# A hybrid decoder layer on one core: the low part of k over zeros, and linear-attention outputs grouped by tiling

## The chip, the cores and the metric

One of the eight cores of a Trainium2 chip runs the whole kernel. The metric is the device time of one execution in microseconds (us); less is better. TensorE (PE) does the matrix products and its weight loads (PEld), VectorE is DVE, ScalarE is ACT, GpSimd is POOL, and SyncE (SP) issues most DMAs.

## What is computed

One layer on 512 tokens of width 1024 in float32: a norm, three token mixers side by side, a gated sum of them, an output projection, and a feed-forward part. Two mixers matter here. Stick-breaking attention (8 heads of 64) and gated linear attention (4 heads, keys of 64, values of 128, chunks of 64 tokens). The attention takes 128 query tokens at a time, with the keys up to their end:

```python
def stick_breaking_attention(q, k, v):
    for i in range(seq // SB_BLOCK):
        ...
        z = jnp.einsum('bhtd,bhsd->bhts', qb, kb) * scale
        ...
        log_1m = jnp.where(mask, jax.nn.log_sigmoid(-z), 0.0)
        tail = lax.cumsum(log_1m, axis=3, reverse=True) - log_1m
        w = jnp.where(mask, jnp.exp(jax.nn.log_sigmoid(z) + tail), 0.0)
        outs.append(jnp.einsum('bhts,bhsd->bhtd', w, vb))
...
def gla_chunked(q, k, v, log_a):
    attn = jnp.where(causal, jnp.einsum('bhntk,bhnsk->bhnts', q_dec, k_inv), 0.0)
    o_intra = jnp.einsum('bhnts,bhnsv->bhntv', attn, v)
...
    o_inter = jnp.einsum('bhntk,bhnkv->bhntv', q_dec, states_before)
    return (o_intra + o_inter).reshape(b, h, s, dv)
```

## The kernel before

Every large product is made of three: each float32 operand is split into a high and a low part of type float32r, and high times high, low times high and high times low are summed in one PSUM bank. Weights come in as 128 x 1024 pieces (512 KB), are split by ACT (line 95) and DVE (line 96), and are used one piece later. Products in plain float32 (transposes, linear attention) need no split; each of those that are not transposes shows in the trace as two records.

PE's program is written out by hand: a feed of projection products (lines 169 to 171 and 100 to 102, all with 128 rows of contraction, 128 stationary columns and 512 moving columns) is handed out piece by piece between the steps of the short chains that wait on other engines. `feed.pull(n)` puts n such products in between.

*The scores of the attention* (`weigh`, lines 589 to 607) run for 8 heads times 4 token blocks, so 32 times. A head has 64 features, half of the 128 rows. Tile `ab` holds, stacked along the rows, q high over q low, and k high twice, so the first product (line 594) makes q high · k high + q low · k high with all 128 rows. The second (line 595) adds q high · k low and uses only the 64 rows of its head (`own`). Block tb takes (tb+1)·128 moving columns, so the 32 steps have 8 each of 128, 256, 384 and 512 columns. Then ACT takes two sigmoids (598, 599), POOL masks (601), DVE runs the product along the keys (604) and one multiplication (606), and a step later PE transposes the result (`turn`, line 616). `k_done` (573 to 583) makes the low part of k of a pair of heads with one DVE subtraction over 128 partitions (579).

*The outputs of the linear attention* (`outputs`, 488 to 517) run four times. A call fills one bank with four pieces of 128 columns, j = 0 to 3 (two token blocks, two heads of the same half e). For each piece comes one product inside the chunks (line 495: 128 rows, 128 columns), and then one for each of its two chunks from the state (line 501: 64 rows, 64 stationary columns, into one half of the partitions). The first chunk of all has no state and is left out, so two calls have 6 products at line 501 and two have 8.

```python
mm(op_[:, o], ats[n0 // 2][:, 4 * e + j, :], gv[:, n, h * P:(h + 1) * P], start=True, stop=False, ...)
for c in (2 * n, 2 * n + 1):
    mm(op_[q0:q0 + 64, o], gq[r, i, c * 64:(c + 1) * 64], st_[r, i, c, :], start=False, stop=True, ...)
```

Small tiles of 128 x 512 float32 come from one pool `tmp` (tag `t2`) with 10 buffers; a scheduler that lays the program out gives a new tile any buffer that is free by then and moves a few instructions within an engine's order.

Of the kernel before, what the change touches and what calls it, by code (L numbers as in the profile page):

```python
# [9 lines left out]
F32 = mybir.dt.float32  # L10
F32R = mybir.dt.float32r
# [5 lines left out]
P = 128  # L17
# [11 lines left out]
class Feed:  # L29
    """Matrix products in the order in which they are to run, handed out piece by piece between the steps of  # L30
    the chains that wait on other engines. A unit is (name, load, body): load() brings the weights in, one
    unit ahead; body(weights) yields after each piece, saying for how many products of 512 columns it stands."""

# [33 lines left out]
def hybrid_layer_kernel(ctx: ExitStack, tc: tile.TileContext, a):  # L67
# [4 lines left out]
    xpool = ctx.enter_context(tc.tile_pool(name="xpool", bufs=1))  # L72
    tmp = ctx.enter_context(tc.tile_pool(name="tmp", bufs=10))
    small = ctx.enter_context(tc.tile_pool(name="small", bufs=6))
# [11 lines left out]

    # ---------------- weights: loaded as float32, split exactly into two float32r parts
    def weights(src, shape, name, parts=None, halves=False):
# [14 lines left out]

    # ---------------- while the first loads run: the activation table, and the tensor engine's clock
    warm = const.tile([P, S], mybir.dt.bfloat16, name="warm")
    nc.gpsimd.memset(warm, 0.0)
# [5 lines left out]

    # ---------------- constants
    g1 = const.tile([P, KD], F32, name="g1")
    nc.sync.dma_start(out=g1, in_=a["mix_pre_g"])

    # ---------------- x, feature-major, times the gain, split
    xTh = xpool.tile([P, KD, S], F32R, tag="aTh", name="xTh")
# [12 lines left out]
    def proj_tm(src, name, done, before=None):  # L131
        """x as the stationary operand: four banks of [128 tokens, 512 columns]."""
        banks = []
# [29 lines left out]
    def proj_fm(src, name, done):  # L163
        """the weights as the stationary operand: a bank of [128 columns, 512 tokens]."""
        def body(w):
            hi, lo = w
            out = bank("acc", f"{name}_ps")
            for k in range(KD):
                mm(out, hi[:, k, :], xTh[:, k, :], start=k == 0, stop=False)  # L169
                mm(out, hi[:, k, :], xTl[:, k, :], start=False, stop=False)  # L170
                mm(out, lo[:, k, :], xTh[:, k, :], start=False, stop=k == KD - 1)  # L171
                if k < KD - 1:
                    yield 3
            done(out)
            yield 3

        feed.add(name, lambda: weights(src, [KD, P], name), body)
# [14 lines left out]

    # ---------------- 1/rms of x: per token-partition, and along the free axis
    ss = small.tile([P, 2, NB], F32, tag="ss1", bufs=1, name="ss")
# [19 lines left out]
    with ExitStack() as mix:  # L214
# [6 lines left out]
        def transposed(src, yh, yl, n, name):  # L221
            """four [128 tokens, 128 features] of block n into the feature-major pair."""
            pt = bank("tv", f"{name}_t{n}")
            for k in range(4):
                nc.tensor.transpose(out=pt[:, k * P:(k + 1) * P], in_=src[k], identity=ident)
            ptv = pt.rearrange("p (k t) -> p k t", k=4)
            t = slice(n * P, (n + 1) * P)
            nc.scalar.activation(yh[:, :, t], ptv, AF.Copy)
            nc.vector.tensor_tensor(out=yl[:, :, t], in0=ptv, in1=yh[:, :, t].bitcast(F32), op=ALU.subtract)

        # ---------------- branch B: spatial gating
        big = mixer.tile([P, 2, NB, S], F32, tag="big", name="sg_uv")
# [21 lines left out]

        # ---------------- what branch C needs first: the low-rank gate, queries and keys
        gla = mix.enter_context(ExitStack())
        gp_ = gla.enter_context(tc.tile_pool(name="gla", bufs=1, side="right"))
        gbias = gp_.tile([P, 2], F32, name="gbias")
        nc.gpsimd.dma_start(out=gbias, in_=a["gla_b_gate"])
        # stacked along the contraction: hi, hi and lo parts of the weights against hi, lo and hi of the gate,  # L260
        # each twice for the two halves that the gate's own product comes in
        gupr = t2("gupr")
        gup = gp_.tile([96, 256], F32R, name="gup")
        for i in range(6):
# [3 lines left out]
                                op=ALU.subtract)  # L268
        # both parts of the low-rank weights side by side as the stationary operand
        gdw = gp_.tile([P, KD, 32], F32R, name="gdw")  # L270
# [44 lines left out]

        # the gate's logarithm, and its running sum in each chunk
        maskg = gp_.tile([P, P], I32, name="maskg")
# [20 lines left out]

        # ---------------- branch B: the spatial mixing
        for gp in range(4):  # L340
# [23 lines left out]

        # ---------------- branch C: gated linear attention
        nc.vector.tensor_tensor(out=la.rearrange("p i (c t) -> p (i c) t", t=64),
# [5 lines left out]
        nc.scalar.activation(dec, cumv[:, :, 63], AF.Exp, scale=1.0 / 16)  # L372
        # two token blocks at a time share one of these
        ats = [x.rearrange("p i (n s) -> p (i n) s", s=P) for x in (la, ex)]
# [18 lines left out]

        # ---------------- gated merge of a branch, two column tiles at a time
        macc = mixer.tile([P, KD, S], F32, tag="macc", name="macc")
# [57 lines left out]
        for i in range(2):  # L453
            # a bank for each of the two row tiles that the chunks' tokens lie in
            ups = [bank("att", f"up{i}{e}") for e in range(2)]
# [20 lines left out]
        def scores(n0):  # L476
            # a bank for each row tile that the heads' features lie in
            for e in range(2):
# [9 lines left out]
        def outputs(n0, e):  # L488
            r = slice(e * 64, e * 64 + 64)
            op_ = bank("att", f"op{n0}{e}")  # L490
            for j in range(4):
                n, i = n0 + j // 2, j % 2
                h = 2 * i + e
                o = slice(j * P, (j + 1) * P)
                mm(op_[:, o], ats[n0 // 2][:, 4 * e + j, :], gv[:, n, h * P:(h + 1) * P], start=True, stop=False,
                   skip_group_check=True)
                for c in (2 * n, 2 * n + 1):
                    if c == 0:
                        continue
                    q0 = (c % 2) * 64  # L500
                    mm(op_[q0:q0 + 64, o], gq[r, i, c * 64:(c + 1) * 64], st_[r, i, c, :],
# [39 lines left out]

        # ---------------- branch A: stick-breaking attention
        feed.to("wp1_3")
        yah, yal = yT("ya")
        with tc.tile_pool(name="attn", bufs=1, side="right") as ap:
# [10 lines left out]
            ab, kl, wts = {}, {}, {}  # L556

            def own_oth(h):
                e = h % 2
                return slice(e * 64, e * 64 + 64), slice(64 - e * 64, 128 - e * 64)  # L560

            # stacked along the contraction: [q hi; q lo] against [k hi; k hi], and q hi against k lo
            def q_done(pq, p):
# [9 lines left out]
            def k_done(pk, p):  # L573
# [3 lines left out]
                nc.scalar.activation(kh, kf, AF.Copy)  # L577
                kl[p] = ap.tile([P, S], F32R, tag="kl", bufs=2, name=f"kl{p}")
                nc.vector.tensor_tensor(out=kl[p], in0=kf, in1=kh.bitcast(F32), op=ALU.subtract)
                for h in (2 * p, 2 * p + 1):  # L580
# [8 lines left out]
            def weigh(h, tb):  # L589
                own, _ = own_oth(h)  # L590
                w = (tb + 1) * P
                t = slice(tb * P, w)
                z = bank("att", f"z{h}{tb}")
                mm(z[:, :w], ab[h][:, 0, t], ab[h][:, 1, :w], start=True, stop=False)
                mm(z[:, :w], ab[h][own, 0, t], kl[h // 2][own, :w], start=False, stop=True)  # L595
                beta = t2(f"be{h}{tb}")
# [90 lines left out]

        # ---------------- token-major residual, and what the FFN needs
        late = ctx.enter_context(tc.tile_pool(name="late", bufs=1, side="right"))
# [17 lines left out]
        with tc.tile_pool(name="mlo", bufs=1, side="right") as mlp:  # L707
# [5 lines left out]

            # ---------------- output projection, norm, residual, norm, transposed
            hTh = xpool.tile([P, KD, S], F32R, tag="aTh", name="hTh")
            hTl = xpool.tile([P, KD, S], F32R, tag="aTl", name="hTl")

            def inv_rms(srcs, junks, name):
# [3 lines left out]
                v = small.tile([P, 1], F32, tag="v2", name="v2" + name)  # L722
                # 1024 (mean + eps); the factor 32 is in the gains
                nc.vector.tensor_scalar(out=v, in0=s2[:, 0:1], scalar1=s2[:, 1:2], scalar2=D * EPS,
# [5 lines left out]
            def after_mixer(n, yb_):  # L730
                """norm and residual of token block n."""
                ys = [t2(f"h{n}{hf}") for hf in range(2)]
# [39 lines left out]

            # the last half of the contraction runs block after block, so that their norms start one by one
            wo = {}
# [36 lines left out]

            # the first pairs run on the first half of the tokens while the second half is still normalized
            first_ps = {fi: bank("acc" if fi[0] else "att", "up%d_ps%d" % fi) for fi in first}
# [7 lines left out]

    # ---------------- convolutional gated FFN
    ffn = ctx.enter_context(tc.tile_pool(name="ffn", bufs=1))
# [65 lines left out]
def _layouts(i):  # L889
    """The inputs as the kernel reads them: slices, transposes and reshapes only."""  # L890
    import numpy as np
# [47 lines left out]
```

## Time and profile before

| | |
|---|---|
| device time, median of 3 runs | 872.11 us (870.83 to 873.0) |
| profiled execution, span from first to last instruction | 872.2 us |
| PE busy | 861.5 us (99%) |
| PE weight loads, DVE, ACT, POOL busy | 698.2, 480.4, 355.8, 89.3 us |
| mean granted clock of PE | 0.997 of full speed |
| DMA | 86.45 MB, mean 99 GB/s |

The page gives no time of the profiled execution apart from its span, and that lies 0.1 us over the median of the runs. Matmuls overlap in the pipeline, so a matmul's own duration is longer than what it costs; the cost is the distance from its start to the start of the next. In the rows a form such as 64*128 is rows times columns of the stationary operand.

### The profile page before, as it was taken

How to read it: one execution, taken by the hardware profiler on the slowest of the kernel's cores; microseconds unless marked ns; L12 is line 12 of the kernel's file. 1: busy time of each engine (PE TensorE's matmuls, PEld its weight loads, DVE VectorE, ACT ScalarE, POOL GpSimd, SP SyncE). 2: the span in 40 equal slices, each digit the busy share in tenths (PEclk: the TensorE clock that was granted, in tenths of full speed). 3: DMA queues.
4: the chain of work that ended last, by engine and by line, in shares of the span. 5: the costliest groups of instructions: out<-in, count | busy, mean ns of one | idle time of the engine just before them, and what ended most of it. 6: DMA issues, size and time to landing. Idle time of an engine off the chain costs nothing.

```text
span 872.2 us, 10327 instructions
## 1 busy us (share of the span) xinstructions
PE 861.5 (99%) x4005; PEld 698.2 (80%) x4005; DVE 480.4 (55%) x652; ACT 355.8 (41%) x536; POOL 89.3 (10%) x137
## 2 busy tenths in 40 slices
PE   8999999999999999999999999999999999999996
PEld 5878877788887777777888898888888888888885
DVE  4358444544266777775664766666666666422225
ACT  6436223322256566554333435444444444311112
POOL 2210003000002332332100120000000000000001
PEclk9999999999999999999999999999999999999999
DMA  8522222122222122222525122232222222222212
GB/s 314 187 69 97 75 94 73 49 97 97 96 91 80 49 73 73 72 73 95 219 97 183 58 73 73 97 97 97 96 97 97 97 97 96 97 97 97 97 49 96
DMA packets 26192, 86.45 MB, mean 99 GB/s; under 512 B 3216, under 2 KB 3712, under 8 KB 26144
## 3 DMA queue, kind: packets, MB, share of 16 engines
q1 hardware_dynamic: 24624, 81.35, 27.2%
q0 software_dynamic: 1520, 4.45, 1.6%
q8 instruction: 31, 0.51, 0.2%
q14 instruction: 17, 0.14, 0.1%
HBM read 83.69 MB, written 2.10 MB: 98 GB/s over the span
## 4 chain that ended last, share of the span: by engine, by line
PE 98%; DMA 1%; SPq 0%; ACT 0%; DVE 0%; issue 0%; POOLq 0%; DVEq 0%; ACTq 0%
PE up_ps L808 9%; PE up_ps L809 9%; PE up_ps L810 9%; PE wg_ps L169 5%; PE wg_ps L171 5%; PE wg_ps L170 5%; PE dn L101 5%; PE dn L100 5%; PE dn L102 5%; PE pp L100 3%; PE pp L102 3%; PE pp L101 3%; PE wo L101 2%; PE wo L102 2%; PE wo L100 2%; PE z L595 1%
## 5 line engine op out<-in xcount | busy, mean ns | idle before, releaser
L809 PE MATMUL up_ps<-hTl,h_wup 128*128 128x512 f32 (+1 forms) x336 | 129.0, 384 | 0.0
L810 PE MATMUL up_ps<-hTh,l_wup 128*128 128x512 f32 (+1 forms) x336 | 129.0, 384 | 0.0
L808 PE MATMUL up_ps<-hTh,h_wup 128*128 128x512 f32 (+1 forms) x336 | 128.9, 384 | 0.0
L96 DVE TENSOR_TENSOR l_wup<-r_wup,h_wup 128x1024 fp32r<-128x1024 f32 x41 | 50.2, 1225 | 64.9 <-ACT h_wup L95 64.9
L169 PE MATMUL wg_ps<-xTh,h_wg 128*128 128x512 f32 x192 | 78.9, 411 | 0.0
L171 PE MATMUL wg_ps<-xTh,l_wg 128*128 128x512 f32 x192 | 75.2, 392 | 0.0
L170 PE MATMUL wg_ps<-xTl,h_wg 128*128 128x512 f32 x192 | 74.9, 390 | 0.0
L808 PEld LDWEIGHTS up_ps<-hTh,h_wup 128*128 128x128 f32 x336 | 63.0, 188 | 12.5
L810 PEld LDWEIGHTS up_ps<-hTh,l_wup 128*128 128x128 f32 x336 | 63.1, 188 | 12.4
L809 PEld LDWEIGHTS up_ps<-hTl,h_wup 128*128 128x128 f32 x336 | 63.1, 188 | 12.4
L96 DVE TENSOR_TENSOR l_wdn<-r_wdn,h_wdn 128x1024 fp32r<-128x1024 f32 x22 | 27.0, 1226 | 82.9 <-ACT h_wdn L95 82.9
L831 DVE SCALAR_TENSOR_TENSOR cv<-up_ps,cw,cv 128x511 f32<-128x511 f32 (+1 forms) x88 | 65.6, 747 | 7.8 <-ACT cv L829 6.2
L101 PE MATMUL dn<-l_wdn,guh 128*128 128x512 f32 x176 | 68.6, 390 | 0.0
L102 PE MATMUL dn<-h_wdn,gul 128*128 128x512 f32 x176 | 68.5, 389 | 0.0
L100 PE MATMUL dn<-h_wdn,guh 128*128 128x512 f32 x176 | 68.4, 389 | 0.0
L95 ACT ACTIVATE h_wdn<-r_wdn 128x1024 fp32r<-128x1024 f32 x22 | 23.3, 1061 | 81.5 <-PE dn L102 79.3
L95 ACT ACTIVATE h_wup<-r_wup 128x1024 fp32r<-128x1024 f32 x41 | 43.5, 1061 | 25.9 <-PE up_ps L809 22.3
L95 ACT ACTIVATE h_wg<-r_wg 128x1024 fp32r<-128x1024 f32 x24 | 25.5, 1062 | 47.4 <-PE wg_ps L170 30.3
L169 PEld LDWEIGHTS wg_ps<-xTh,h_wg 128*128 128x128 f32 x192 | 36.1, 188 | 9.1 <-issue 1.9
L171 PEld LDWEIGHTS wg_ps<-xTh,l_wg 128*128 128x128 f32 x192 | 36.0, 188 | 8.0
L170 PEld LDWEIGHTS wg_ps<-xTl,h_wg 128*128 128x128 f32 x192 | 36.2, 188 | 6.3
L604 DVE TENSOR_TENSOR_SCAN re<-re 128x128 f32<-128x128 f32 (+3 forms) x32 | 27.2, 851 | 24.7 <-POOL re L601 24.3
(413 smaller groups left out, 1764.2 us busy)
## 6 DMA issues: line engine op xcount, KB each, us to landing
r_wup<-in_ffn_w_up SPq DMA_DIRECT2D x44, 512.0 KB, 3.2
r_wg<-in_w_gate SPq DMA_DIRECT2D x24, 512.0 KB, 3.2
r_wdn<-in_ffn_w_down SPq DMA_DIRECT2D x22, 512.0 KB, 3.2
r_wo<-in_w_out SPq DMA_DIRECT2D x8, 512.0 KB, 3.3
xT<-in_xT SPq DMA_DIRECT2D x8, 256.0 KB, 8.0
xr<-in_x SPq DMA_DIRECT2D x8, 256.0 KB, 5.7
r_wsv<-in_w_sv SPq DMA_DIRECT2D x4, 512.0 KB, 6.1
r_wgv<-in_w_gv SPq DMA_DIRECT2D x4, 512.0 KB, 3.2
```

The costliest lines, as they stand in the source:

```text
L95: nc.scalar.activation(hi[:, p], raw[:, p], AF.Copy)
L96: nc.vector.tensor_tensor(out=lo[:, p], in0=raw[:, p], in1=hi[:, p].bitcast(F32), op=ALU.subtract)
L100: mm(out, lh, rh, start=start, stop=False)
L101: mm(out, lh, rl, start=False, stop=False)
L102: mm(out, ll, rh, start=False, stop=stop)
L169: mm(out, hi[:, k, :], xTh[:, k, :], start=k == 0, stop=False)
L170: mm(out, hi[:, k, :], xTl[:, k, :], start=False, stop=False)
L171: mm(out, lo[:, k, :], xTh[:, k, :], start=False, stop=k == KD - 1)
L808: mm(pu[:, t], hi[:, k, :], hTh[:, k, t], start=k == 0, stop=False, skip_group_check=True)
L809: mm(pu[:, t], hi[:, k, :], hTl[:, k, t], start=False, stop=False, skip_group_check=True)
L810: mm(pu[:, t], lo[:, k, :], hTh[:, k, t], start=False, stop=k == KD - 1, skip_group_check=True)
L831: nc.vector.scalar_tensor_tensor(out=o[:, j:], in0=pu[:, :S - j], scalar=cw[:, c, 2 - j:3 - j], in1=o[:, j:], op0=ALU.mult, op1=ALU.add)
```

## The change

In `weigh` the second product uses all 128 rows too: its stationary operand is the whole of `ab` (q high over q low), and its moving operand is a tile `klz` in which the low part of k stands in the head's own 64 rows and zeros in the others. There are four such tiles (two pairs of heads in turn, two heads each), zeroed once by POOL; `k_done` fills two of them with two DVE subtractions of 64 partitions instead of one of 128. In `outputs` all four products inside the chunks come first, then the state's products into the lower half of the partitions, then those into the upper half. The pool `tmp` has 9 buffers instead of 10, and the tile for the warm-up products at the start is taken from it. Comments are dropped, which moves no line.

```diff
-    tmp = ctx.enter_context(tc.tile_pool(name="tmp", bufs=10))
+    tmp = ctx.enter_context(tc.tile_pool(name="tmp", bufs=9))
...
-    warm = const.tile([P, S], mybir.dt.bfloat16, name="warm")
+    warm = tmp.tile([P, S], mybir.dt.bfloat16, tag="t2", name="warm")
...
                 mm(op_[:, o], ats[n0 // 2][:, 4 * e + j, :], gv[:, n, h * P:(h + 1) * P],
-                   start=True, stop=False,
+                   start=j == 0, stop=False,
                    skip_group_check=True)
-                for c in (2 * n, 2 * n + 1):
+            for q0 in (0, 64):
+                for j in range(4):
+                    n, i = n0 + j // 2, j % 2
+                    o = slice(j * P, (j + 1) * P)
+                    c = 2 * n + q0 // 64
                     if c == 0:
                         continue
-                    q0 = (c % 2) * 64
                     mm(op_[q0:q0 + 64, o], gq[r, i, c * 64:(c + 1) * 64], st_[r, i, c, :],
...
+            klz = [[ap.tile([P, S], F32R, name=f"klz{j}{e}") for e in range(2)] for j in range(2)]
+            for j in range(2):
+                nc.gpsimd.memset(klz[j][0][64:128, :].bitcast(F32), 0.0)
+                nc.gpsimd.memset(klz[j][1][0:64, :].bitcast(F32), 0.0)
...
-                kl[p] = ap.tile([P, S], F32R, tag="kl", bufs=2, name=f"kl{p}")
-                nc.vector.tensor_tensor(out=kl[p], in0=kf, in1=kh.bitcast(F32), op=ALU.subtract)
+                kl[p] = klz[p % 2]
+                for e in range(2):
+                    r = slice(e * 64, e * 64 + 64)
+                    nc.vector.tensor_tensor(out=kl[p][e][r], in0=kf[r], in1=kh[r].bitcast(F32), op=ALU.subtract)
...
-                mm(z[:, :w], ab[h][own, 0, t], kl[h // 2][own, :w], start=False, stop=True)
+                mm(z[:, :w], ab[h][:, 0, t], kl[h // 2][h % 2][:, :w], start=False, stop=True)
```

PE, the second call of `outputs` (tokens 0 to 255, odd heads): `op` is its bank, `gla_vr` holds the values, `la` the masked scores, `state` and `gq` the state and the queries. A line with - is the order before, with + the order now.

```order
-L495 MATMUL op_1138<-gla_vr,la 128x128
-L501 MATMUL op_1138<-state,gq 64x128
-L495 MATMUL op_1138<-gla_vr,la 128x128
-L501 MATMUL op_1138<-state,gq 64x128
-L495 MATMUL op_1138<-gla_vr,la 128x128
-L501 MATMUL op_1138<-state,gq 64x128 x2
-L495 MATMUL op_1138<-gla_vr,la 128x128
-L501 MATMUL op_1138<-state,gq 64x128 x2
+L495 MATMUL op_1138<-gla_vr,la 128x128 x4
+L504 MATMUL op_1138<-state,gq 64x128 x6
```

Four alternations between the two forms become one. The other three calls change in the same way (two with x8 in the last row), and at the scores PE's order is as it was.

DVE around the low part of k of heads 4 and 5, before: `kf` and `kh` are k and its high part, `wa2l` a low part of head 2's transposed weights, `ab` the low part of q, `l_wp_1` a weight piece.

```order
L575 TENSOR_TENSOR kf_2318<-wk_ps,rsb 128x512
L96 TENSOR_TENSOR l_wp_1_2402<-r_wp_1_2400,h_wp_1_2401 128x1024
L579 TENSOR_TENSOR kl_2322<-kf_2318,kh_2320 128x512
L624 TENSOR_TENSOR wa2l<-wt_2328,wa2h 128x2x128
L570 TENSOR_TENSOR ab_2236<-qf_2231,ab_2236 64x512
L604 SCALAR_TENSOR_TENSOR re_2350<-re_2350 128x512
```

The same place now:

```order
L583 TENSOR_TENSOR kf_2326<-wk_ps,rsb 128x512
L96 TENSOR_TENSOR l_wp_1_2410<-r_wp_1_2408,h_wp_1_2409 128x1024
L589 TENSOR_TENSOR klz_1610<-kf_2326,kh_2328 64x512
L589 TENSOR_TENSOR klz_1611<-kf_2326,kh_2328 64x512
L578 TENSOR_TENSOR ab_2244<-qf_2239,ab_2244 64x512
L633 TENSOR_TENSOR wa2l<-wt_2336,wa2h 128x2x128
L613 SCALAR_TENSOR_TENSOR re_2358<-re_2358 128x512
```

One subtraction has become two, and the low part of q comes ahead of the low part of the weights. On ACT and SP no instruction has moved; POOL gets the four memsets ahead of the last reciprocal root of the linear attention's norm.

## Rows read from the trace of the kernel before

**Rows 1.** The page: busy time of each engine, and the chain that ended last.
```profile
PE 861.5 (99%) x4005; PEld 698.2 (80%) x4005; DVE 480.4 (55%) x652; ACT 355.8 (41%) x536; POOL 89.3 (10%) x137
...
PE 98%; DMA 1%; SPq 0%; ACT 0%; DVE 0%; issue 0%; POOLq 0%; DVEq 0%; ACTq 0%
```
**Rows 2.** Waits of PE's weight loads: waiting line, reason: us in total, times, longest.
```profile
PEld z L595 <- issue: 8.8, 32, 0.4
```
**Rows 3.** Timeline of PE, 128-column step: start us, us, engine, line, out<-in, form.
```profile
255.11 0.22 PE L594 MATMUL z<-ab 128*128 128x128 f32 x1
255.26 0.32 PE L595 MATMUL z<-kl,ab 64*128 64x128 f32 x1
255.51 0.49 PE L169 MATMUL wq_ps<-xTh,h_wq 128*128 128x512 f32 x1
255.84 0.39 PE L170 MATMUL wq_ps<-xTl,h_wq 128*128 128x512 f32 x1
256.07 0.40 PE L171 MATMUL wq_ps<-xTh,l_wq 128*128 128x512 f32 x1
```
**Rows 4.** Timeline of PE, a step of 256 columns and one of 512.
```profile
258.39 0.28 PE L594 MATMUL z<-ab 128*128 128x256 f32 x1
...
259.24 0.39 PE L170 MATMUL wk_ps<-xTl,h_wk 128*128 128x512 f32 x1
...
303.37 0.39 PE L594 MATMUL z<-ab 128*128 128x512 f32 x1
...
304.44 0.40 PE L170 MATMUL wg_ps<-xTl,h_wg 128*128 128x512 f32 x1
```
**Rows 5.** Timeline of PE, three short products of 128 rows in a row.
```profile
297.99 0.22 PE L637 MATMUL av<-wb1h,vst 128*128 128x128 f32 x1
...
298.10 0.30 PE L616 MATMUL wt<-ident,be 128*128 128x128 f32 x1
298.16 0.48 PE L169 MATMUL wk_ps<-xTh,h_wk 128*128 128x512 f32 x1
298.48 0.39 PE L170 MATMUL wk_ps<-xTl,h_wk 128*128 128x512 f32 x1
```
**Rows 6.** Timeline of PE, the second and the third call of outputs.
```profile
145.22 0.38 PE L495 MATMUL op<-gla_vr,la 128*128 128x128 f32 x2
145.53 0.43 PE L501 MATMUL op<-state,gq 64*64 64x128 f32 x2
145.89 0.49 PE L495 MATMUL op<-gla_vr,la 128*128 128x128 f32 x2
...
147.08 0.44 PE L501 MATMUL op<-state,gq 64*64 64x128 f32 x4
...
148.23 0.50 PE L169 MATMUL wg_ps<-xTh,h_wg 128*128 128x512 f32 x1
...
160.74 0.38 PE L495 MATMUL op<-gla_vr,ex 128*128 128x128 f32 x2
...
163.77 0.50 PE L100 MATMUL pp<-ybh,h_wp 128*128 128x512 f32 x1
```
**Rows 7.** Timeline of PE: four transposes; sixteen records in two row tiles, and the next.
```profile
176.60 0.60 PE L225 MATMUL yc_t<-ident,osq 128*128 128x128 f32 x4
...
123.91 1.71 PE L484 MATMUL ap<-gq,ki 64*128 64x128 f32 x16
125.54 0.50 PE L100 MATMUL wgr_ps<-h_wgr,xTh 128*128 128x512 f32 x1
```
**Rows 8.** Timelines of DVE and of PE: head 2's last block, and its transposes.
```profile
309.72 0.68 DVE L606 TENSOR_TENSOR be<-be,re 128x511 f32<-128x511 f32 x1
...
311.29 0.60 PE L616 MATMUL wt<-ident,be 128*128 128x128 f32 x4
```
**Rows 9.** Timeline of POOL: the last reciprocal root of the linear attention.
```profile
171.38 1.01 POOL L191 TENSOR_TENSOR ro<-so,expo 128x4 f32<-128x4 f32 x1 [4.89 <-DVE so L507]
```
**Rows 10.** The page: one group of weight loads (last: us busy, mean ns).
```profile
L808 PEld LDWEIGHTS up_ps<-hTh,h_wup 128*128 128x128 f32 x336 | 63.0, 188 | 12.5
```

More of the change, by code (lines that the diff above doesn't have):

```diff
@@ L494, in outputs @@
                 o = slice(j * P, (j + 1) * P)
-                mm(op_[:, o], ats[n0 // 2][:, 4 * e + j, :], gv[:, n, h * P:(h + 1) * P], start=True, stop=False,
+                mm(op_[:, o], ats[n0 // 2][:, 4 * e + j, :], gv[:, n, h * P:(h + 1) * P], start=j == 0, stop=False,
                    skip_group_check=True)
-                for c in (2 * n, 2 * n + 1):
+            for q0 in (0, 64):
[3 more added lines that the diff above has]
+                    c = 2 * n + q0 // 64
                     if c == 0:
                         continue
-                    q0 = (c % 2) * 64
                     mm(op_[q0:q0 + 64, o], gq[r, i, c * 64:(c + 1) * 64], st_[r, i, c, :],
@@ L589, in weigh @@
             def weigh(h, tb):
-                own, _ = own_oth(h)
                 w = (tb + 1) * P
```

## The prediction

> **What bounds the kernel now.** I read the page first. PE is busy 99% of the span and the chain that ended last is PE to 98% [rows 1], so nearly every microsecond that PE's stream gets shorter should come off the end, as long as no other engine takes over. I then asked where PE's weight loads wait: before the second product of the scores they sit idle 32 times, 8.8 us in total, and the reason is no engine but "issue" [rows 2]. Such a wait is inside PE. So I went through PE's timeline and measured from start to start, since the durations overlap.
>
> A product of the feed, 128 rows and 512 columns, costs 0.23 us (255.84 to 256.07) [rows 3]. In a step of the scores with 128 columns the first product holds PE for 0.15 us, the second, with 64 rows, for 0.25, and the feed product behind it for 0.33 instead of 0.23 [rows 3]. Short products that stay on 128 rows are far cheaper: two of 128 columns start within 0.11 us (297.99 to 298.10), and the third is followed after 0.06 [rows 5]. The difference is the step from 128 rows to 64 and back: PE empties, and the next weights are loaded in the open. The same stands at each alternation in the outputs of the linear attention [rows 6].
>
> **The change, part by part.** The sum is made against the profiled execution: span 872.2 us, 0.1 over the median, so I set the two equal.
>
> *The scores.* I measure from the first product's start to the start of the second feed product behind. Before: 255.84 - 255.11 = 0.73 us for 128 columns [rows 3], 0.85 for 256 and 1.07 for 512 [rows 4]. After, all of it has 128 rows. 512 columns: three products of 0.23, 0.69; saved 0.38. 256: two halves of 0.23, then 0.23, 0.46; saved 0.39. For 128 columns two products of 0.06 are too short to hide the loads behind them: after three such products the following feed product takes 0.32 (298.16 to 298.48) [rows 5]. So 0.12 + 0.32 = 0.44; saved 0.29. I take 384 columns like 512. With 8 steps of each: 8 x (0.29 + 0.39 + 0.38 + 0.38) = 11.5 us. The upper bound has the loads hidden at 128 columns too (0.1 x 8 more), 12.3; the lower is a rival below. That half of the rows multiply zeros costs nothing by these rows: a product's price goes by its columns.
>
> *The outputs.* Before, the second call takes 148.23 - 145.22 = 3.01 us, the third 163.77 - 160.74 = 3.03 [rows 6]. After, each has eight records inside the chunks, one step to the 64-row form, the state's records, one step back. Plain-float32 records of 128 columns in one form come every (0.60 - 0.27)/3 = 0.11 us (four records in 0.60, the last lasting 0.27) [rows 7]. Two such records and the step to 64 rows take 0.31 (145.22 to 145.53) [rows 6], so eight and the step take 6 x 0.11 + 0.31 = 0.97.
>
> What the state's records then cost turns on one question, whether those of the two halves of the partitions run side by side. Now they do: two records take 0.43 us and four, two for each half, 0.44 [rows 6]. That holds while neighbours lie in different halves; the change puts up to eight of one half in a row. The nearest rows are the sixteen records of the masked scores, eight in one row half and then eight in the other: 125.54 - 123.91 = 1.63 us with the way back [rows 7]. One half alone would take 0.36 (145.53 to 145.89) for two records and the way back [rows 6], and 6 x 0.11 more, 1.02; both one after the other 0.36 + 14 x 0.11 = 1.90. So the 1.63 is partly side by side, and I take it for the calls with eight products: 3.03 - 0.97 - 1.63 = 0.43 saved. The calls with six have four records, then eight: between 1.02 and 0.36 + 10 x 0.11 = 1.46; with so few ahead I take 1.1: 3.01 - 0.97 - 1.1 = 0.94 saved. I price the first call, whose first product stands apart, like the second. Sum: 2 x 0.43 + 2 x 0.94 = 2.7 us. All serial: 2 x 0.16 + 2 x 0.58 = 1.5. All side by side: 4 x 1.03 = 4.1.
>
> The Trainium skill has a rule here, in "TensorE: Matmul & The Clock Gate", Part 3: matmuls are in strict order in start and end, with no reordering. By that rule the second half's records could begin only after the first half's last had begun, and grouping would be the serial case. Here the trace speaks against so strict an order, for sixteen records in two groups took 1.63 us.
>
> *The low part of k.* Four DVE subtractions become eight; one over as many columns takes about 0.68 us [rows 8], so 0.7 us more on DVE for each of the four pairs, on an engine that is busy 55% [rows 1]. What could be late is the turn of an even head's last block, whose chain stands behind the copies of `k_done` on ACT: head 2's result is ready at 309.72 + 0.68 = 310.40, and PE wants it at 311.29, a margin of 0.89 us [rows 8]. Between the block whose DVE pass the chain follows and this turn PE gets three steps faster, 0.38 + 0.38 + 0.29 = 1.05, of which 0.09 (0.15 - 0.06) comes to the chain as well. That leaves about 0.1 us too little, in the three even heads that have a pair behind them: 0.3 us given back. The low part of q is now ahead of the weights' low part on DVE; the bank that this frees is wanted only by the turn after next, so I price it at nothing. If that cover went, one 0.7 us pass would show, three times.
>
> *Memsets, buffers.* POOL zeroes four tiles before the last root, in the 4.89 us in which it waited [rows 9]. Were the root late, 172.39 of its end to 176.60 of the transposes [rows 7, 9] is 4.2 us, less one DVE pass of about 0.7: 3.5 us of cover. With nine small buffers for ten, the fullest moment of the attention holds q, k, k high, one y, two weights and one rest, seven; I price it at nothing. At the start the warm-up tile holds one of nine until the warm-up products are through, before the x rows ask for it; nothing.
>
> Sum: 11.5 + 2.7 - 0.3 = 13.9 us, so 872.1 - 13.9 = **858.2 us**.
>
> **The rivals.** *Serial halves.* Grouping loses the side-by-side running: 1.5 instead of 2.7, time 859.4. For it: the records of one half wait in a row. Against: the 1.63 us.
>
> *Loads in the open.* The padded product sits on the same rows as the first, and if weights could load only while another part of the array multiplies, each of two loads per step would show, 0.1 us (0.33 - 0.23) each: 32 x 0.2 = 6.4 us less, of which the 128-column steps have 8 x 0.1 in the sum already; 858.2 + 5.6 = 863.8. Against it: a 128-column weight load lasts 0.19 us [rows 10] and yet full products follow each other every 0.23 [rows 3]. The Trainium skill says so in the same Part 3: weight loads overlap matmuls only when the row group differs. By that rule this rival would hold.
>
> *The step is not the rows.* The 0.15 and 0.25 could belong to a second product into the same bank. Then only the outputs gain: 872.1 - 2.7 = 869.4. Against: the feed sums 24 products into a bank at 0.23.
>
> *Slower: late turns.* With nine buffers the sigmoids of a step wait for a tile that the turn before still holds, and each of 32 turns finds its weights late. The place is ACT's line 598. It decides from 13.9/32 = 0.43 us per turn; at 1 us each, 858.2 + 32 = 890. For it: a margin of 0.89 us at head 2. Against: seven tiles held of nine.
>
> **How the numbers follow.** Forecast 0.68 (own range 856 to 859), serial halves 0.12, loads in the open 0.08, gains beyond my bounds (below 855.5) 0.05, not the rows 0.05, late turns 0.02. The last three are what the range leaves out in part: low 855.5 is all side by side with hidden loads, 872.1 - 12.3 - 4.1 = 855.7, and a little spread; high 862.5 takes in the serial case and half of the open loads (861). A measurement tells about 0.3%, 2.6 us, from no change. All cases but late turns are faster, and 869.4 is so close to the bound that I halve it: faster 0.95, same 0.03, slower 0.02.
>
> **What would show it.** Right: in the scores first and second product follow at 0.06 to 0.23 us by their columns, the feed product behind takes 0.23 (0.33 only at 128 columns), and the idle time of the second product's weight loads falls from 8.8 us to almost nothing. In the outputs a call takes about 2.6 us with eight products and 2.1 with six; 2.9 and 2.4 would be the serial case. PE stays near 99%. Wrong: weight loads idle before both products of a step (open loads), the feed product still at 0.33 behind 256 and 512 columns, or PE waiting for `wt` at line 625 for more than 0.3 us in all (late turns).

## The result, and the profile after

The change is faster: 859.43 us (median of four runs, 858.46 to 861.14) against 871.47 us (four runs, 870.3 to 873.0) in the same comparison, a ratio of 0.9854 with a 95% interval of 0.9836 to 0.9872. That is 12.0 us by the medians and 12.7 by the ratio. A second, later comparison gave 15.5 and 15.2 us (below). The forecast was 858.2 us.

The profiled execution has a span of 856.8 us and a granted clock of 0.998, against 872.2 and 0.997: 15.4 us. In each run shown the time lies 1.7 us over the span (858.46 against 856.8 here).

First the page, busy time and the chain that ended last, as [rows 1]:

```profile
PE 846.2 (99%) x4005; PEld 697.7 (81%) x4005; DVE 483.0 (56%) x656; ACT 354.1 (41%) x536; POOL 86.0 (10%) x141
...
PE 92%; issue 4%; POOL 1%; DMA 1%; DVE 1%; ACT 1%; SPq 0%; POOLq 0%; DVEq 0%; ACTq 0%
```

PE's instructions are as many as before (4005) and it is still busy 99% of the span, so what is gone is time between starts, not products. The chain that ended last, 98% PE before, now leaves PE for 23 us ahead of each of two late turns (heads 2 and 4, below). DVE has four instructions and 2.6 us more: the four added subtractions.

Next the waits of PE's weight loads (waiting line, reason: us in total, times, longest), as [rows 2]. The 8.8 us before the second product of the scores have no row any more. A new one stands instead, the transposes of three turns:

```profile
PEld wt L625 <- ACT be L608: 1.4, 3, 0.6
```

PE's timeline (start, us, engine, line, out<-in, form), one step of the scores with 128 columns and one with 512, as [rows 3, 4]:

```profile
250.38 0.22 PE L603 MATMUL z<-ab 128*128 128x128 f32 x1
250.44 0.28 PE L604 MATMUL z<-klz,ab 128*128 128x128 f32 x1
250.55 0.45 PE L169 MATMUL wq_ps<-xTh,h_wq 128*128 128x512 f32 x1
250.84 0.40 PE L170 MATMUL wq_ps<-xTl,h_wq 128*128 128x512 f32 x1
...
259.80 0.39 PE L603 MATMUL z<-ab 128*128 128x512 f32 x1
260.03 0.39 PE L604 MATMUL z<-klz,ab 128*128 128x512 f32 x1
260.26 0.40 PE L169 MATMUL wg_ps<-xTh,h_wg 128*128 128x512 f32 x1
260.49 0.39 PE L170 MATMUL wg_ps<-xTl,h_wg 128*128 128x512 f32 x1
```

With 512 columns the three products follow at 0.23 us each (259.80, 260.03, 260.26, 260.49). With 128 columns the first holds PE for 0.06 us, the second for 0.11 and the feed product behind for 0.29: 0.46 us in all, where it was 0.73.

Two calls of `outputs`, six and eight products from the state, as [rows 6]:

```profile
142.45 1.05 PE L495 MATMUL op<-gla_vr,la 128*128 128x128 f32 x8
143.44 1.10 PE L504 MATMUL op<-state,gq 64*64 64x128 f32 x12
144.46 0.50 PE L169 MATMUL wg_ps<-xTh,h_wg 128*128 128x512 f32 x1
...
157.01 1.05 PE L495 MATMUL op<-gla_vr,ex 128*128 128x128 f32 x8
158.00 1.58 PE L504 MATMUL op<-state,gq 64*64 64x128 f32 x16
159.50 0.50 PE L100 MATMUL pp<-ybh,h_wp 128*128 128x512 f32 x1
```

They take 144.46 - 142.45 = 2.01 us and 159.50 - 157.01 = 2.49, where they took 3.01 and 3.03. Last, the turn of head 2's last block on DVE and on PE, as [rows 8] (in brackets the idle time before and what ended it; the sigmoid on ACT that is named was over by 300.13, so what released it must be the last writer of `be`, the DVE pass shown):

```profile
301.50 0.68 DVE L615 TENSOR_TENSOR be<-be,re 128x511 f32<-128x511 f32 x1
...
301.78 0.39 PE L171 MATMUL wg_ps<-xTh,l_wg 128*128 128x512 f32 x1
302.33 0.63 PE L625 MATMUL wt<-ident,be 128*128 128x128 f32 x4 [0.16 <-ACT be L608]
302.71 0.47 PE L169 MATMUL wg_ps<-xTh,h_wg 128*128 128x512 f32 x1
```

DVE ends at 301.50 + 0.68 = 302.18, and the transposes begin 0.15 us later. The feed product before them started 0.55 us earlier instead of 0.23, and the step behind them is 0.03 longer: 0.35 us lost here.

**Where the time came from**, from start to start, over all steps of each kind (mean of 8 steps for each width, first product to second feed product behind):

| | before | after | saved, all of them |
|---|---|---|---|
| scores, 128 columns | 0.74 | 0.45 | 2.3 |
| scores, 256 columns | 0.85 | 0.47 | 3.1 |
| scores, 384 columns | 0.97 | 0.58 | 3.1 |
| scores, 512 columns | 1.08 | 0.69 | 3.1 |
| outputs, first call | 2.71 | 1.79 | 0.9 |
| outputs, second call | 3.02 | 2.01 | 1.0 |
| outputs, third and fourth call | 3.03 each | 2.49 each | 1.1 |
| late turns (heads 0, 2, 4) | 0 | 0.12, 0.35, 0.35 | -0.8 |

The sum is 11.6 + 3.0 - 0.8 = 13.8 us, between the two comparisons (12.7 and 15.2 by their ratios). The other 1.6 us of the two profiled spans are not the change's places; they lie at the start, where PE waits for the first tile of x, 1.94 us in the profile before and 1.36 after. Behind that wait the granted clock differs, as a window over the same stretch shows (before, then after; us, PE busy with its records, granted clock, share and GB/s of the DMA):

```profile
13.30:16.20 2.90, 2.90 (x8) 0.50 1.03 406
13.30:16.20 2.90, 2.90 (x14) 1.00 1.03 404
```

At 0.50 (1.2 GHz) the products follow each other at 0.43 us, at 1.00 (2.4 GHz) at 0.23. PE's 37th record, behind all this, starts at 17.76 us before and at 16.02 after: 1.7 us, before any place of the change. From that record to the end the spans are 854.5 and 840.7 us, 13.7 apart, as the sum has it. The change is not what sets that wait, as far as profiles show: a second one of the changed kernel waited 2.23 us and also ran at 0.50 behind it.

### The profile page after: what moved, and what is told of

It reads as the page before. It is cut to its first block, busy times and chain, and to the rows that moved or that the text cites. A ratio compares the mean times of both kernels' runs of the same rounds, so it can differ in the third digit from the quotient of the medians.

```text
span 856.8 us, 10352 instructions
## 1 busy us (share of the span) xinstructions
PE 846.2 (99%) x4005; PEld 697.7 (81%) x4005; DVE 483.0 (56%) x656; ACT 354.1 (41%) x536; POOL 86.0 (10%) x141
## 4 chain that ended last, share of the span: by engine, by line
PE 92%; issue 4%; POOL 1%; DMA 1%; DVE 1%; ACT 1%; SPq 0%; POOLq 0%; DVEq 0%; ACTq 0%
PE up_ps L818 9%; PE up_ps L819 9%; PE up_ps L817 9%; PE dn L101 5%; PE wg_ps L169 5%; PE dn L100 5%; PE dn L102 5%; PE wg_ps L171 5%; PE wg_ps L170 5%; PE pp L100 3%; PE pp L102 3%; PE pp L101 3%; PE wo L101 2%; PE wo L102 2%; PE wo L100 2%
## 5 line engine op out<-in xcount | busy, mean ns | idle before, releaser
L101 PEld LDWEIGHTS dn<-l_wdn,guh 128*128 128x128 f32 x176 | 33.0, 188 | 7.0 <-DVE l_wdn L96 0.3
```

The source lines that it names most:

```text
L101: mm(out, lh, rl, start=False, stop=False)
```

## The experiments

Each stands beside runs of the kernel before on the same chip. The theory: the time went with the visits to the 64-row form, 11.5 us of them in the scores and 2.7 in the outputs, less 0.3 for late turns.

**The scores alone.** The changed kernel with the loop of `outputs` as it was.

```diff
-                   start=j == 0, stop=False,
+                   start=True, stop=False,
-            for q0 in (0, 64):
-                for j in range(4):
-                    ...
+                for c in (2 * n, 2 * n + 1):
+                    ...
```

> The changed kernel with the loop of the outputs put back as it was (product inside the chunk, then its two state products, piece by piece). Step theory (the price is the step between the 128-row form and a narrower one): the scores save 8 x (0.29 + 0.39 + 0.39 + 0.39) = 11.6 us as in the changed kernel, late turns give 0.7 back, the calls of the outputs take 3.0 us again; 10.9 us under the kernel before. Rival (most of the gain comes from the outputs or from the new buffers): under 6 us.

Measured: 861.1 us against 872.58, ratio 0.9882 (0.9864 to 0.99), so 10.3 us by the ratio. Its steps of the scores are those of the changed kernel to 0.002 us, and the three late turns are there too (0.12, 0.35, 0.35). 11.6 - 0.8 = 10.8 us by the trace. The scores and the late turns come together, without the grouping.

**The grouping alone.** The kernel before with the new loop of `outputs`.

```diff
-                   start=True, stop=False,
+                   start=j == 0, stop=False,
-                for c in (2 * n, 2 * n + 1):
-                    ...
+            for q0 in (0, 64):
+                for j in range(4):
+                    ...
```

> The kernel before with the grouped loop of the outputs alone. Step theory: calls of 2.0 us (six state products) and 2.5 us (eight) for 3.0, together 3.1 us under the kernel before; the steps of the scores keep 0.74 to 1.08 us and no turn waits. Rival (grouping helps only because the scores became faster): nothing.

Measured: 869.15 us, ratio 0.9963 (0.9949 to 0.9977), so 3.2 us by the ratio. PE's timeline of the third call:

```profile
157.34 1.05 PE L495 MATMUL op<-gla_vr,ex 128*128 128x128 f32 x8
158.32 1.58 PE L504 MATMUL op<-state,gq 64*64 64x128 f32 x16
159.83 0.50 PE L100 MATMUL pp<-ybh,h_wp 128*128 128x512 f32 x1
```

2.49 us as in the changed kernel, and no turn is late. The parts add up: 0.9882 and 0.9963 multiply to 0.9845, and both together gave 0.9854.

**Alternating halves.** The changed kernel with two loops exchanged, so that the state's products go to the lower and the upper half of the partitions in turn, still after all four products inside the chunks.

```diff
-            for q0 in (0, 64):
-                for j in range(4):
+            for j in range(4):
+                for q0 in (0, 64):
```

> The changed kernel with the state's products in turn into the lower and the upper half of the partitions, still after all four products inside the chunks. If the two halves run side by side whenever neighbours differ, the calls with eight state products fall from 2.49 to 2.0 us and those with six stay at 2.0: 1.0 us under the changed kernel. Rival (records run strictly in order, the gain of grouping is only the fewer steps): no change, or 2.9 us per call.

PE's timeline of the third call:

```profile
159.75 1.05 PE L495 MATMUL op<-gla_vr,ex 128*128 128x128 f32 x8
160.73 1.09 PE L504 MATMUL op<-state,gq 64*64 64x128 f32 x16
161.75 0.50 PE L100 MATMUL pp<-ybh,h_wp 128*128 128x512 f32 x1
```

The sixteen records take 161.75 - 160.73 = 1.02 us instead of 1.50, the price that the prediction worked out for one half alone from [rows 6], and a call 2.00 instead of 2.49. The calls with six products gain 0.01. So the grouped order runs only partly side by side, and this one fully: 1.0 us more over four calls. The time, 858.12 us (ratio 0.9838, 0.9822 to 0.9853), is too coarse for 1 us: this profile waits 3.9 us for the first tile of x. Behind the start it is 1.0 us shorter (table below).

**Nine buffers alone.** The kernel before with nine buffers and the warm-up tile among them.

```diff
-    tmp = ctx.enter_context(tc.tile_pool(name="tmp", bufs=10))
+    tmp = ctx.enter_context(tc.tile_pool(name="tmp", bufs=9))
-    warm = const.tile([P, S], mybir.dt.bfloat16, name="warm")
+    warm = tmp.tile([P, S], mybir.dt.bfloat16, tag="t2", name="warm")
```

> The kernel before with nine small buffers and the warm-up tile taken from them, nothing else. Step theory and the count of seven tiles held: no change, within 1 us. Rival (nine buffers make sigmoids wait for the turn before): slower by 1 us or more, with waits of ACT for tiles at line 598 and of PE at line 616.

Measured: 872.09 us (twelve runs) against 872.58 (nineteen), ratio 0.9998 (0.9986 to 1.001). No wait of the sigmoids was added: they wait 18.9 us for PE's scores in 18 places, as against 18.8 in 18. The waits that the slower rival needs are not there, and a cost of the buffer, if any, is under the 1 us of the interval.

**The second product twice.** The kernel before with the product at line 595 issued twice in a row. It adds the low part of k twice.

```diff
                 mm(z[:, :w], ab[h][own, 0, t], kl[h // 2][own, :w], start=False, stop=...)
+                mm(z[:, :w], ab[h][own, 0, t], kl[h // 2][own, :w], start=False, stop=True)
```

> The kernel before with line 595, the 64-row product of the scores, issued twice in a row, so that the low part is added twice. Step theory: the second of the two is already in the 64-row form and costs its columns only, 0.11, 0.12, 0.17 and 0.23 us: 8 x 0.63 = 5.0 us slower. Rival (the price sits on each 64-row product, or on each further product into a bank, as 0.25 to 0.43 us apiece): 8 x (0.25 + 0.31 + 0.37 + 0.43) = 10.9 us slower.

Measured: 876.43 us against 872.75, ratio 1.0048 (1.0031 to 1.0066), so 2.7 to 5.8 us more. PE's timeline, a 128-column step:

```profile
252.82 0.22 PE L594 MATMUL z<-ab 128*128 128x128 f32 x1
252.97 0.32 PE L595 MATMUL z<-kl,ab 64*128 64x128 f32 x1
253.13 0.27 PE L596 MATMUL z<-kl,ab 64*128 64x128 f32 x1
253.34 0.49 PE L169 MATMUL wq_ps<-xTh,h_wq 128*128 128x512 f32 x1
253.67 0.39 PE L170 MATMUL wq_ps<-xTl,h_wq 128*128 128x512 f32 x1
```

The step takes 253.67 - 252.82 = 0.85 us instead of 0.74: a second product into the same bank, again with 64 rows, adds 0.11 us; over the four widths 0.11, 0.12, 0.17 and 0.24, or 8 x 0.65 = 5.2 us. The change saved 0.29 to 0.39 per step while it kept a second product in the same bank. So the cost was not that of a second product: it is paid once for a visit to 64 rows, and a neighbour of the same form pays about its columns.

**Late turns moved.** The alternating version, with three feed products moved from behind the turn of a head's last block to ahead of it (the first number of each row of `STEP`).

```diff
-STEP = ((12, 6, 6, 9), (9, 6, 6, 6))
+STEP = ((15, 6, 6, 9), (6, 6, 6, 6))
```

> As e3 with three feed products moved from behind the turn to ahead of it in the first step of each head (12 and 9 become 15 and 6). If the three late turns come only from the margin of 0.15 us that the faster scores leave, PE's waits at the transposes (0.7 us in all, 0.24 each) go, and the time is 0.7 us under e3. Rival (a fixed delay behind each such turn, whatever stands ahead): they stay.

Measured: 855.56 us against 872.75, ratio 0.9819 (0.98 to 0.9838). DVE and PE at head 2's last block:

```profile
298.80 0.68 DVE L615 TENSOR_TENSOR be<-be,re 128x511 f32<-128x511 f32 x1
...
300.57 0.39 PE L171 MATMUL wg_ps<-xTh,l_wg 128*128 128x512 f32 x1
300.81 0.60 PE L625 MATMUL wt<-ident,be 128*128 128x128 f32 x4
```

The result is there at 299.48 and PE takes it at 300.81. All eight turns of a last block now start 0.23 us after the product before, and the row of waits at line 625 is gone. What was lost at the turns was lateness and not a fixed delay behind ACT.

**Both again, side by side.** The changed kernel and the version just shown, on one chip.

> The changed kernel once more, beside e7 on one chip: by the sum of its trace (11.6 in the scores, 3.1 in the outputs, 0.7 given back) 14.0 us under the kernel before, ratio 0.984. If the first median of 12.0 us less was nearer, ratio 0.986.

> The kernel of e6 once more, beside the changed kernel: 1.0 us less in two calls of the outputs and 0.7 us less at three turns, 1.7 us under a_again, ratio to the kernel before 0.982. Rival (nothing is left of it in the time): the same as a_again.

Measured: the changed kernel 856.99 us (five runs), the other 855.79 (four runs), the kernel before 872.51; ratios 0.9826 (0.9806 to 0.9846) and 0.9809 (0.9792 to 0.9826). The trace has the last version 1.0 us better in the outputs and 0.8 in the turns; by medians it is 1.2 us better. The intervals overlap, so that it beats the change is shown by the trace and only suggested by the time of whole runs. The late turns were the same in this second profile of the changed kernel (0.12, 0.35, 0.35).

**The profiles without their start.** With the start left out, as in the result above, the profiled spans compare far more closely than the times: the changed kernel twice within 0.05 us, the last version twice within 0.01.

| kernel | PE's wait for x | 37th record starts | from there to the end | against before |
|---|---|---|---|---|
| before | 1.94 | 17.76 | 854.5 | |
| nine buffers alone | 2.87 | 18.09 | 854.6 | +0.1 |
| second product twice | 1.19 | 15.47 | 859.6 | +5.1 |
| grouping alone | 2.23 | 16.34 | 851.5 | -3.0 |
| scores alone | 1.18 | 15.56 | 843.7 | -10.7 |
| changed kernel, and again | 1.36, 2.23 | 16.02, 16.29 | 840.7, 840.8 | -13.7, -13.7 |
| alternating halves | 3.92 | 18.76 | 839.8 | -14.7 |
| late turns moved, and again | 0.10, 2.33 | 14.56, 16.53 | 839.1, 839.1 | -15.4, -15.4 |

Each agrees to about 0.2 us with what the starts at its own places add up to (in the same order 0, 5.2, 3.0, 10.8, 13.8, 14.8 and 15.6 us).

## Why the prediction was right, point by point

**The sum, 13.9 forecast, 13.8 by the trace,** is nearer than its parts: the outputs saved 0.3 us more than forecast and the late turns gave back 0.5 more. That these two misses nearly cancel is luck.

**The scores, 11.5 forecast, 11.6 measured.** Each width came out as priced: 0.29, 0.39, 0.39 and 0.39 saved, against 0.29, 0.39, 0.38 and 0.38. The loads that stay in the open at 128 columns were taken from three short products in a row [rows 5], and that was the right row for the sum (0.45 us, 0.44 forecast). Inside it the split was another: the second product holds PE for 0.11 us and not 0.06, the feed product behind for 0.28 and not 0.32.

**Loads in the open** is ruled out. Three products over all 128 rows follow each other at 0.23 us, while their loads last 0.19 each [rows 10]. The rule of the Trainium skill ("TensorE: Matmul & The Clock Gate", Part 3) that loads overlap only where the row group differs doesn't hold in these traces: the row group is the same. (The same Part of the Trainium skill names an exception beside that rule, weights that are loaded into a background buffer; no run here tells whether that is at work.) What the trace bears out, for the 64-row form, is another sentence of it, in "TensorEngine Tiling (Array Packing)", Key Properties: changing the tiling mode drains the engine. A visit to 64 rows cost 0.29 to 0.39 us here; the last section has changes of form that cost nothing.

**The step is not the rows** is ruled out too, by the product issued twice and by the changed scores themselves.

**The outputs, 2.7 forecast, 3.0 measured.** The eight records inside the chunks and the step took 158.00 - 157.01 = 0.99 us (0.97 forecast). The term that was mis-sized is that of the state's records with eight products: I took 1.63 us from the masked scores, and they took 1.50, so 0.54 was saved per call and not 0.43. With six products they took 144.46 - 143.44 = 1.02, the bound for one half alone, not 1.1; 1.0 was saved, not 0.94. The serial case (1.90 and 1.46) is ruled out. How the two halves overlapped is to be seen when the group of 16 records is cut by time, in two windows of PE's timeline that end at 158.47 and at 158.85:

```profile
158.00 0.65 PE L504 MATMUL op<-state,gq 64*64 64x128 f32 x4
...
158.00 1.08 PE L504 MATMUL op<-state,gq 64*64 64x128 f32 x11
```

Four records had begun by 158.47, and seven more began in the next 0.38 us, where one half alone, at 0.11 each, has room for three or four. So the second half starts beside the last records of the first. By the rule of the Trainium skill weighed in the prediction (no reordering of starts) it would have begun only after all eight, and the records would have taken 1.90; this order of starts disagrees with it. Which half a record belongs to is not in the trace: it is inferred from these distances and from the order in which the kernel's code issues the products.

**Late turns, 0.3 forecast, 0.8 measured.** The mechanism was right, the three even heads with a pair behind them, and the size was off. The step that failed is "That leaves about 0.1 us too little". I set the margin of 0.89 us against PE's 1.05, less 0.09 that comes to the chain. But of the margin 0.15 was never free: the transposes begin that long after DVE's end, as head 2 after the change shows. 1.05 - (0.89 - 0.15) = 0.31, and measured were 0.32 and another 0.03 in the step behind. The 0.09 of relief was not seen at heads 2 and 4: from the first score product of the head's 384-column block to the result of its last block, head 2 took 10.77 us in both profiles, 299.63 to 310.40 before and 291.41 to 302.18 after. At head 0 this stretch fell from 10.71 to 10.53 us, and only 0.12 was lost. The sign that the prediction had set for late turns did show: PE's waits at line 625 come to 0.3 us and those of its weight loads to 1.4. It was tied to the nine buffers, though, and these alone changed nothing; with the feed products moved the waits are gone, still with nine buffers.

**The low part of k** costs what was said on DVE and nothing on PE. One row of DVE shows both halves, 0.7 us each, and they lie ahead of a wait of DVE's that POOL ends:

```profile
296.38 1.38 DVE L589 TENSOR_TENSOR klz<-kf,kh 64x512 fp32r<-64x512 f32 x2
...
300.05 1.23 DVE L613 TENSOR_TENSOR_SCAN re<-re 128x512 f32<-128x512 f32 x1 [1.13 <-POOL re L610]
```

DVE still idles 1.13 us before the product along the keys, so its longer work is hidden there, now with 0.8 us less to spare than the 1.92 it idled at this place before. What made the turns late is PE's earlier demand, not this work.

**The memsets** were rightly priced at nothing, though not for the whole reason given. They were to run in the 4.89 us in which POOL waited [rows 9]. POOL's timeline shows that they had to wait for the last products of the outputs:

```profile
165.09 0.52 POOL L563 MEMSET klz<- 64x512 f32 x1 [2.87 <-PE op L504]
...
166.80 0.52 POOL L564 MEMSET klz<- 64x512 f32 x1
167.29 1.00 POOL L191 TENSOR_TENSOR ro<-so,expo 128x4 f32<-128x4 f32 x1
```

The root had its input from DVE at 166.77 and began at 167.29, 0.5 us late. The transposes that need it came at 171.88, 3.6 us after its end, where 4.2 were before; so the second reason, the cover behind the root, carried it.

**The span.** "I set the two equal" was not right: the time lies some 1.7 us over the span in all runs whose span is listed (2.0 in one). If that held for the profiled execution of the kernel before, it was about 873.9 us, some 2 us above the median. The saving was taken from 872.1, which was also the median, so the forecast was not moved by it. That two comparisons of the same pair give 12.7 and 15.2 us goes with the granted clock of the runs. In the profile before it was 0.91 in the first 20 us and 1.00 from there to 840 us, in the profile after 1.00 in both. The changed kernel's four runs of the first had means of 0.995 to 0.998, three of its five in the second 0.999. Over all comparisons with a clock listed, runs at the same mean differ by 13.8 us at 0.996 (873.0 us, the mean of eight before; 859.2 of three after) and by 14.2 at 0.999 (871.1 of six; 856.9 of three), about the 13.8 of the trace, and by 13.0 to 13.3 at the other three values, where the changed kernel has one run each. The clocks of the kernel before in the first comparison are not on record.

## What to carry to other kernels

A lone product with 64 rows between products with 128 is dear for its two changes of form, not for its work; where zeros are free to keep, pad it to the form of its neighbours, and otherwise put all products of the small form together. Where products of two halves stand together, let the halves alternate in the program's order, for that ran fully side by side where two groups ran so only in part. To measure a change of a few us, compare profiles from a fixed record behind the start to the end: here that brought two profiles of one kernel within 0.05 us, where whole runs spread by 3. When PE gets faster, compare the gain between two fixed points with the margin of each chain that ends there, less the time between the last result and its use.

## What was not expected of the hardware

The price sits on few changes of form. Neither 32 stationary columns nor 96 rows show it. PE's timeline of the kernel before has both:

```profile
56.06 0.40 PE L285 MATMUL gd_ps<-xTh,gdw 128*32 128x512 f32 x1
56.30 0.40 PE L286 MATMUL gd_ps<-xTl,gdw 128*32 128x512 f32 x1
...
65.24 0.63 PE L330 MATMUL lg<-gds,gup 96*128 96x512 f32 x2
65.71 0.39 PE L169 MATMUL wgq_ps<-xTh,h_wgq 128*128 128x512 f32 x1
65.94 0.40 PE L170 MATMUL wgq_ps<-xTl,h_wgq 128*128 128x512 f32 x1
```

Two records with 96 rows take 65.71 - 65.24 = 0.47 us, twice a full product's 0.23, and the product behind them 0.23 as well; with 32 stationary columns the distance is 0.24. Both are free of the step that the 64-row form pays between products of 512 columns [rows 4]. The other surprise is how much the order within a bank of products matters: the same sixteen records took 1.50 us in two groups of eight and 1.02 in turn.
